# One encoder block on Trainium2: the work around the output projection goes to VectorE, weights are read earlier, and second products start from a copy of the first

## The chip, the cores and the metric

One core of one Trainium2 chip runs the whole program. The metric is the device time of one execution in microseconds (us), taken as the median of several runs. TensorE (PE) multiplies matrices out of SBUF into PSUM, which has eight banks of 128 x 512 fp32 numbers. VectorE (DVE), ScalarE (ACT) and GpSimd (POOL) work element by element; POOL does not touch PSUM. SyncE (SP) starts the transfers between the chip's main memory and SBUF. Each engine works through its own queue in order, and semaphores hold an instruction until what it needs is there.

## The reference

The input is 1024 tokens of width 1024, in front of which 16 meta tokens are set; all numbers are fp32. Two kinds of attention run in parallel on the normed input (four heads of differential attention, branch A; eight heads of windowed attention with sinks, branch B). They are merged by gates, projected, and followed by a SwiGLU feed-forward network (FFN) of width 2816:

```
merged = sigmoid(ga) * (y_a @ w_ba) + sigmoid(gb) * (y_b @ w_bb)     # 1024 x 512 @ 512 x 1024, twice
h = h + merged @ w_o                                                 # 1024 x 1024 @ 1024 x 1024
h = h + (silu(n @ w_gate) * (n @ w_up)) @ w_down                     # n = rms_norm(h, norm_ffn)
return rms_norm(h, norm_final)[:, N_META:]
```

The change touches the lines of the merge, of `w_o`, and of the first half of the FFN.

## The kernel before, in words

**Split numbers.** TensorE gets each fp32 operand as a high part and a low part. ScalarE copies the operand into the high part (rounded, line 112), and another engine, VectorE or POOL as the call says, subtracts that from the operand to make the low part (line 113). Both are done by `split(hi, lo, src, lo_eng)`. A product is then three matmuls: high by high, high by low, low by high. One matmul here is 128x128 by 128x512.

**Seven products for eight.** The projection and the FFN's products cut each matrix in quarters and use seven products of quarters in place of eight (Winograd's form). With the left side A (the merged rows) and the right side W: P1 = a11 w11, P2 = a12 w21, P6, P5 and P7 multiply sums of quarters, P3 and P4 a quarter by a sum. P1 + P2 is one quarter of the result; P6, P7 and P4 are added into the bank that holds P1, P3 into that which holds P5. The sums are element by element work for VectorE and POOL.

**Branches.** For each o of 0 to 7 (128 columns of the merge) and each half (512 tokens), `gated` reads a gate from main memory, takes its sigmoid and multiplies y by a 128-column piece of the branch's weights (12 matmuls) into a PSUM bank. Branch B runs first, with its result times the gate stored into a quarter (`merged(o, half)`); then branch A, in the order `order_a`, with its result times the gate (VectorE, line 887) added on POOL (line 888). `load_wo` reads quarters of `w_o`, 1 MB each.

**Output projection.** `right_o(p, j)` and `left_o(p, j)` split the two sides of product p, step j; `left_t` does so for the left side of P7 and P4. The steps run P1, P2, P6, P5, P3, four steps of four banks (`set1`, `set2`, `sets_o[5]`) and three matmuls each; then P7 and P4 bank by bank (`product_t`). After a product's last step, `out_add` (line 921) adds its banks to the rows `h2`. `ahead(n)` prepares the operands eight steps before they are used. When a block of 128 rows is complete, `norm_f` norms it, and `turn_f` transposes it on TensorE into two PSUM banks ("a turn"), from which ScalarE and VectorE make the FFN's operands, high and low part. Turns 0 to 4 stand between the last products of the projection (`TURN_O`), turns 5 to 7 among the first FFN products (`TURN`). From the second half of the tokens, a turn also makes the sums for P5, P6, P7 and P4 (lines 1080 to 1084), which `split_t` splits.

**FFN, first half.** The 2816 columns are 11 blocks fp of 256; i is 0 for the gate's weights and 1 for the up weights. `weights` reads and sums a block's weights and splits them, `product_f` multiplies (12 matmuls for each of seven p) into the banks b1, b2 and b3. For fp 0 to 3 (N_EARLY) P1 and P2 of all come first, since they need only half of the tokens, and the rest later; there the order for fp 1 to 3 is P1, P2 of i = 0, then P1, P2 of i = 1. From fp 4 on it is P1 of both i, P2 of both i, and so on. For fp below N_KEPT P1's bank is kept until P6 is added; for the others ScalarE copies P1 to SBUF and back. `result` evacuates: silu for i = 0, a multiplication with it for i = 1.

**Order.** On TensorE the order of the program text is kept. For the other engines and for SP a planner simulates the program and writes each engine's queue in the order in which its simulation starts the instructions. Buffers of one tag go round: a tile waits until the readers of the one before it in the same place are done. All PSUM tiles of these stages have one tag with eight banks:

```
def ps_bank(name):
    return bank(psum3, "bank", name, 8)
```

The functions that the diff touches, with the line numbers of the profile:

Of the kernel before, what the change touches and what calls it, by code (L numbers as in the profile page):

```python
# [60 lines left out]
S_TMP = 2  # L61
C_BUFS = 8
STAGGER = 3
# [7 lines left out]
def encoder_block(ctx: ExitStack, tc: tile.TileContext, x, meta, norm_mix, w_in, lq1, lk1, lq2, lk2,  # L71
# [746 lines left out]
    def ya(j, b, tk):  # L818
        return ya_t[j][:, b] if tk.start else ya0[:, b, j]

    def load_wo(w, row, col):
# [31 lines left out]
    late_pool, close_late = pool("late_pool", "right")  # L853
    gffn = row(late_pool, norm_ffn, D, "gffn")
    first_f = [late_pool.tile([P, 1024], F32, name=f"first_f{i}") for i in range(2)]
    w21 = late_pool.tile([P, 4, 512], F32, name="w21")
    load_wo(w21, 1, 0)


    tt_v, tt_p = nc.vector.tensor_tensor, nc.gpsimd.tensor_tensor  # L860
    t2 = [None, None]
    rights, lefts = {}, {}

    def right_o(p, j):
        if p == 6:
            src = t2[j // 2][:, j % 2 * 512:j % 2 * 512 + 512]
        else:
            src = w11[:, j] if p in (1, 5) else w21[:, j] if p in (2, 4) else m2[:, (3, 7).index(p), j]
        ob = rights[p, j] = late_pool.tile([P, 2, 512], F32R, tag="ob_o", name=f"ob_o{p}_{j}", bufs=8)
        split(ob[:, 0], ob[:, 1], src, nc.vector)  # L870

    def left_o(p, j):
        oa = lefts[p, j] = op_tile(f"oa_o{p}_{j}")
        split(oa[:, 0], oa[:, 1], {1: a11, 2: a12, 6: a11, 5: asum, 3: a12}[p][:, j], nc.gpsimd)

    def left_t(p, u):

        oa = lefts[p, u] = op_tile(f"oa_o{p}_{u}").rearrange("p a (c n) -> p a c n", n=P)
        split(oa[:, 0], oa[:, 1], {7: a21, 4: a22}[p][:, :, u * P:(u + 1) * P], nc.gpsimd)


    order_a = [(o, 0) for o in range(6)] + [(0, 1), (6, 0), (1, 1), (7, 0)] + [(o, 1) for o in range(2, DC)]
    for n, (o, half) in enumerate(order_a):
# [4 lines left out]
        nc.gpsimd.tensor_tensor(merged(o, half), gt, merged(o, half), ALU.add)  # L888
        if n < 4:
            right_o(1, n)  # L890
        elif n < 8:
            right_o(2, n - 4)
            left_o(1, n - 4)
        elif n < 12:
            if n > 9:
                left_o(2, n - 10)
        elif n < 14:
            left_o(2, n - 10)
            if n == 12:
                m2 = block_pair(2, "m2", F32)  # L900
                w22, w12 = m2[:, 0], m2[:, 1]
                load_wo(w12, 0, 1)
                load_wo(w22, 1, 1)
    close_ya()
    close_ypool()


    h2pool, close_h2 = pool("h2pool")

    def h2_tile(name):  # L910
# [3 lines left out]
    for t in range(NT):  # L914
        h2.append(h2_tile(f"h2_{t}"))
        nc.sync.dma_start(h2[t], x[t * P:(t + 1) * P, :])
    h2_d = [dram.tile([P, D], F32, name=f"h2_d{t}") for t in range(NT)]

# [136 lines left out]
    def turn_f(t):  # L1055
# [5 lines left out]
        for b in range(2):  # L1061
            pt = four(ps_bank(f"ptn_f{t}_{b}"))
            for c in range(4):
# [38 lines left out]
    set2 = [ps_bank(f"po_2_{u}") for u in range(4)]  # L1102
    sets_o = {1: set1, 2: set2, 6: set1}

    def product_o(p, j, u):
        oa, ob = lefts[p, j], rights[p, j]
        for k, (a, b) in enumerate(((0, 0), (0, 1), (1, 0))):
            nc.tensor.matmul(sets_o[p][u], oa[:, a, u * P:(u + 1) * P], ob[:, b, :],  # L1108
                             start=(p in (1, 2, 5) and j == 0 and k == 0),
                             stop=(p in (2, 3) and j == 3 and k == 2), skip_group_check=True)  # L1110
# [8 lines left out]
    def ahead(n):  # L1119
# [5 lines left out]
        else:  # L1125
            right_o((7, 4)[n // 4 - 3], n % 4)
            left_t(*((7, 0), (7, 1), (4, 0), (4, 1), (7, 2), (7, 3), (4, 2), (4, 3))[n - 12])

    for n, (p, j) in enumerate(steps_o):
        if (p, j) == (5, 0):  # L1130
            sets_o[5] = sets_o[3] = [ps_bank(f"po_5_{u}") for u in range(4)]
# [11 lines left out]
        for k in (n - 1, n) if last else (n,):  # L1143
            ahead(k)
            if k < 4:
                tt_v(a12[:, k], a12[:, k], a11[:, k], ALU.subtract)
            elif k < 8:
                tt_p(w21[:, k - 4], w21[:, k - 4], t2[(k - 4) // 2][:, k % 2 * 512:k % 2 * 512 + 512], ALU.subtract)
            elif k < 12:
# [3 lines left out]
    for n, (p, u) in enumerate(((7, 0), (7, 1), (4, 0), (4, 1), (7, 2), (7, 3), (4, 2), (4, 3))):  # L1153
        product_t(p, u)
# [5 lines left out]
    prepare(2 * 2)  # L1160
    close_late()
    close_keep()

# [22 lines left out]
    def product_f(fp, p, i):  # L1186
# [4 lines left out]
        late = N_KEPT <= fp < N_EARLY  # L1191
        if p in (1, 2, 5) or (late and p == 6):
            u[which] = ps_bank(f"pg_{nm}_{p}")
        ps = u[which]
# [3 lines left out]
        for c in range(4):  # L1198
            for n, (x, y) in enumerate(((0, 0), (0, 1), (1, 0))):
                nc.tensor.matmul(ps, op[:, x, c, :], b[:, y, c, :], start=(p in (1, 2, 5) and c == 0 and n == 0),  # L1200
                                 stop=(p in (4, 2, 3) and c == 3 and n == 2), skip_group_check=True)
        g = st.setdefault(("c", fp), {})

        def result(key, src, other=None):
# [8 lines left out]
            else:  # L1213
                if other is not None:
                    both = p_tile(f"p2_{nm}") if late and key == "11" else other
                    nc.vector.tensor_tensor(both, src, other, ALU.add)
                    src = both
                nc.vector.tensor_tensor(g[key], g[key], src, ALU.mult)

        if p in (1, 5):  # L1220
            u[p] = p_tile(f"p{p}_{nm}")
            nc.scalar.copy(u[p], ps)
# [64 lines left out]
    def product_d(p, j, us_):  # L1287
        oa, ob = ops["d", (p, j)]
        if BANKS[p] not in sets:
            sets[BANKS[p]] = [ps_bank(f"pd_{p}_{u}") for u in range(4)]  # L1290
        ps = sets[BANKS[p]]
# [127 lines left out]
```

## Time and profile before

| | us |
|---|---|
| median of 3 runs | 1462.16 (1461.48 to 1463.27) |
| the profiled execution | 1462.58 |
| its span, first to last instruction | 1460.8 |
| TensorE busy | 1435.5 (98%) |
| VectorE busy | 925.3 (63%) |
| ScalarE busy | 673.4 (46%) |
| POOL busy | 553.2 (38%) |
| mean granted TensorE clock | 0.995 of full speed |

In the rows of the profile, L12 is line 12 of the kernel; `m<-gt,m` is a tile written from two tiles (numbers left out); x4 is a count. A bracket behind a row of the order of time gives how long the engine stood before it, and which instruction ended that. PE is TensorE's matmuls and PEld its weight loads, which overlap them. A matmul's shown duration is longer than the pace, since one begins before the last has ended.

### The profile page before, as it was taken

Reading aid. Unit: us, or ns where it says so; the run is one execution under the profiler, and the core shown is the slowest. Engines: PE = TensorE matmul, PEld = TensorE weight load, DVE = VectorE, ACT = ScalarE, POOL = GpSimd, SP = SyncE. Lnnn points to the kernel's source line nnn. Section 1 sums busy time; section 2 is a strip of 40 time slices with the busy share of each in tenths; the row PEclk is TensorE's granted clock in tenths of the full one; section 3 lists DMA queues with packets and bytes.
Section 4 is the critical chain, followed back from the end, with each engine's and each line's share of the span. In section 5 each row is a group of like instructions: output and inputs, shape, how many; then the busy total and the mean of one; then the engine's idle time right before and its main releaser. Section 6 shows DMA issues by size and latency. Waiting matters only on the chain.

```text
span 1460.8 us, 21057 instructions
## 1 busy us (share of the span) xinstructions
PE 1435.5 (98%) x7327; PEld 1230.6 (84%) x7327; DVE 925.3 (63%) x1724; ACT 673.4 (46%) x1267; POOL 553.2 (38%) x512
## 2 busy tenths in 40 slices
PE   8999999999999999999989989999999999999997
PEld 7998989988898999888878868888888888788886
DVE  7456326628686868436698876655555554787667
ACT  6356336525555556355335633433333333444454
POOL 4143223313323232222876365554444542000444
PEclk9999999999999999999999999999999999999999
DMA  7334452372424251096421623432233323954333
GB/s 238 91 96 114 120 128 88 77 223 83 146 74 145 74 153 66 37 304 215 144 101 79 174 95 115 144 124 100 99 104 107 102 94 108 347 191 140 124 126 141
DMA packets 158618, 191.02 MB, mean 131 GB/s; under 512 B 16096, under 2 KB 103584, under 8 KB 158512
## 3 DMA queue, kind: packets, MB, share of 16 engines
q1 hardware_dynamic: 158512, 189.68, 40.6%
q8 instruction: 58, 0.95, 0.3%
q14 instruction: 48, 0.39, 0.1%
HBM read 129.14 MB, written 53.94 MB: 125 GB/s over the span
## 4 chain that ended last, share of the span: by engine, by line
PE 82%; DVE 6%; issue 4%; POOL 4%; DMA 2%; ACT 1%; SPq 1%; POOLq 0%; DVEq 0%; ACTq 0%
PE pg L1200 26%; PE pp_g L200 11%; PE pd L1294 8%; PE aps L607 4%; PE apy L649 3%; PE pp_va L200 3%; PE pp_ka L200 3%; PE pp_qb L200 3%; PE pp_qa L200 3%; POOL oa L113 3%; PE po L1108 2%; PE ppa L551 2%; PE apt L636 2%; PE bpt L338 2%; PE bpy L344 2%
## 5 line engine op out<-in xcount | busy, mean ns | idle before, releaser
L1200 PE MATMUL pg<-t,wop 128*128 128x512 f32 x1056 | 242.4, 389 | 0.0
L1200 PEld LDWEIGHTS pg<-t,wop 128*128 128x128 f32 x1056 | 198.2, 188 | 41.2
L113 POOL TENSOR_TENSOR wop<-wf,wop 128x512 fp32r<-128x512 f32 x122 | 165.7, 1360 | 172.6 <-ACT wop L112 161.7
L1294 PE MATMUL pd<-ob,oa 128*128 128x512 f32 x924 | 210.2, 389 | 1.5 <-DVE ob L113 1.1
L1294 PEld LDWEIGHTS pd<-ob,oa 128*128 128x128 f32 x924 | 173.3, 188 | 38.2 <-DVE ob L113 1.5
L1200 PE MATMUL pg<-b,wop 128*128 128x512 f32 x792 | 186.2, 393 | 5.2 <-ACT ts L1084 3.3
L1200 PEld LDWEIGHTS pg<-b,wop 128*128 128x128 f32 x792 | 149.3, 189 | 38.0 <-ACT ts L1084 3.7
L113 POOL TENSOR_TENSOR wl_c<-w_c,wh_c 128x1024 fp32r<-128x1024 f32 x32 | 77.7, 2427 | 162.5 <-ACT wh_c L112 138.3
L112 ACT ACTIVATE wop<-wf 128x512 fp32r<-128x512 f32 x128 | 80.5, 633 | 79.8 <-PE pg L1200 53.9
L113 POOL TENSOR_TENSOR oa<-ra,oa 128x512 fp32r<-128x512 f32 x33 | 44.1, 1336 | 171.4 <-ACT oa L112 170.0
L618 ACT ACTIVATE as<-as,amn 128x1040 f32<-128x1040 f32 x64 | 74.5, 1165 | 72.7 <-DVE amn L613 72.4
L200 PE MATMUL pp_g<-hT_hi,wh_c 128*128 128x512 f32 x256 | 101.3, 396 | 0.0
L200 PE MATMUL pp_g<-hT_lo,wh_c 128*128 128x512 f32 x256 | 100.9, 394 | 0.0
L200 PE MATMUL pp_g<-hT_hi,wl_c 128*128 128x512 f32 x256 | 100.9, 394 | 0.0
L112 ACT ACTIVATE oa<-ra 128x512 fp32r<-128x512 f32 x77 | 48.6, 632 | 107.8 <-PE pd L1294 52.7
L607 PE MATMUL aps<-ak,aq 128*128 128x352 f32 (+1 forms) x384 | 92.6, 326 | 0.0
L607 PEld LDWEIGHTS aps<-ak,aq 128*128 128x128 f32 x384 | 69.6, 188 | 14.0
L974 DVE TENSOR_TENSOR s<-wf,wf 128x512 f32<-128x512 f32 x20 | 18.3, 916 | 96.7 <-DMA wf<-in_w_ff_up_dram 53.3
L613 DVE CUSTOM_DVE_ANT_0 as<-aps,dist,amn 128x352 f32<-128x352 f32 (+1 forms) x128 | 71.2, 563 | 10.2 <-PE aps L607 8.1
L325 POOL TENSOR_SCALAR bs<-bs,bdn 128x432 f32<-128x432 f32 (+1 forms) x64 | 37.1, 601 | 87.6 <-DVE bdn L323 65.3
L621 POOL TENSOR_SCALAR as<-as,adn,neglam 128x1040 f32<-128x1040 f32 x32 | 39.0, 1219 | 75.2 <-DVE adn L619 75.2
L315 DVE CUSTOM_DVE_ANT_0 bs<-bps,tbx,nsink 128x432 f32<-128x432 f32 (+1 forms) x64 | 38.4, 624 | 41.6 <-PE bps L313 38.5
(275 smaller groups left out, 3134.8 us busy)
## 6 DMA issues: line engine op xcount, KB each, us to landing
ra<-aop SPq DMA_DIRECT2D x77, 256.0 KB, 2.6
w_c<-in_w_in_dram SPq DMA_DIRECT2D x33, 512.0 KB, 4.1
wf<-in_w_ff_gate_dram SPq DMA_DIRECT2D x25, 512.0 KB, 3.6
wf<-in_w_ff_up_dram SPq DMA_DIRECT2D x25, 512.0 KB, 3.6
aop<-as SPq DMA_DIRECT2D x44, 256.0 KB, 2.1
aop<-c SPq DMA_DIRECT2D x33, 256.0 KB, 2.0
g_d<-gate_stage SPq DMA_DIRECT2D x32, 256.0 KB, 2.0
gt<-g_d SPq DMA_DIRECT2D x32, 256.0 KB, 3.7
```

The costliest lines, as they stand in the source:

```text
L112: nc.scalar.activation(hi, src, AF.Copy)
L113: lo_eng.tensor_tensor(lo, src, f32(hi), ALU.subtract)
L200: nc.tensor.matmul(ps[:, :n], a[:, c, :], b[:, c, at:at + n], start=(c == 0 and i == 0), stop=(c == DC - 1 and i == 2))
L315: nc.vector.tensor_tensor_reduce(st[:, r, :W], ps[:, :W], tb, 2.0 ** -(4 * g + r + 1), nsink[:, 4 * g + r:4 * g + r + 1], ALU.add, ALU.min ...
L325: nc.gpsimd.tensor_scalar(st[:, r, :W], st[:, r, :W], dn[:, r:r + 1], 1.0, ALU.mult, ALU.mult)
L607: nc.tensor.matmul(ps[:, :n], qs[m][:, t * P:(t + 1) * P], ks[m][:, vv, k0:k0 + n], start=(vv == 0), stop=(vv == 1))
L613: nc.vector.tensor_tensor_reduce(s[m][:, a:b], ps[:, a - k0:b - k0], far_by, slope, low, ALU.add, ALU.min, mn[:, m, i + j:i + j + 1])
L618: nc.scalar.activation(s[m][:, 0:L], s[m][:, 0:L], AF.Exp, bias=low, scale=-1.0, accum_out=dn[:, m:m + 1])
L621: (nc.gpsimd if t % 4 in COMBINE_POOL else nc.vector).tensor_scalar(s[1][:, 0:L], s[1][:, 0:L], dn[:, 1:2], neglam, ALU.mult, ALU.mult)
L649: nc.tensor.matmul(py[:, cols], v[:kp, a, k, :], at_[:kp, k, b, :], start=(k == 0 and j == 0), stop=(k == 8))
L1200: nc.tensor.matmul(ps, op[:, x, c, :], b[:, y, c, :], start=(p in (1, 2, 5) and c == 0 and n == 0), stop=(p in (4, 2, 3) and c == 3 and n ...
L1294: nc.tensor.matmul(ps[u], oa[:, a, u * P:(u + 1) * P], ob[:, b, :], start=(p in (1, 2, 5) and j == 0 and k == 0), stop=(p in (2, 3, 4) and ...
```

## The change

- **Reads.** All four quarters of `w_o` but w22 are read beside branch B (w11 after o = 3, w12 after 4, w21 after 5). P1's right side is split there too, and w11 becomes w12 - w11 there, both on VectorE.
- **Sums and low parts.** The sums of the merged quarters are made beside branch A on VectorE, as they become complete, in another form (a21 = a11 - a21, asum = a22 - a21, a11 = asum + a11). All low parts of the projection's left sides, which were POOL's, are VectorE's, and so are the sums of fp 0 and the low parts of P1 and P2 for fp 2 and 3. w21's update goes from POOL to VectorE and to later steps.
- **Second products.** When P1 of the projection is complete, ScalarE copies its four banks to P2's, and P2 is added to that copy; the separate add of P1 to the rows goes. In the FFN's first half, P1 is copied to P2's bank (fp 0, 1 and from 4 on), or P2 is added in P1's own bank after that was copied to SBUF (fp 2 and 3), and the add of the two results goes.
- **Banks.** PSUM is divided: six banks of the old tag, and two of a new tag for half 1 of the branches, half of P2's and P5's banks in the projection, the turns, P5 in the FFN and half of one set in its second half. N_KEPT goes from 3 to 2.
- **Order.** The last products of the projection run 7,0 7,1 7,2 4,0 7,3 4,1 4,2 4,3 in place of 7,0 7,1 4,0 4,1 7,2 7,3 4,2 4,3, and the turns 0 to 3 stand one product later. The FFN norm's weights and the first FFN weights are read after branch A, into a pool of their own; copies of P5 and P6 are in another pool, of 16 buffers in place of 8.

```diff
 def ps_bank(name):
-    return bank(psum3, "bank", name, 8)
+    return bank(psum3, "bank", name, 6)
+
+def ps_bank_t(name):
+    return bank(psum3, "bank_t", name, 2)
...
+wopool, close_wo = pool("wopool", "right")
+w12, w21 = (wopool.tile([P, 4, 512], F32, name=f"w{n}") for n in ("12", "21"))
...
 def left_o(p, j):
     oa = lefts[p, j] = op_tile(f"oa_o{p}_{j}")
-    split(oa[:, 0], oa[:, 1], {1: a11, 2: a12, 6: a11, 5: asum, 3: a12}[p][:, j], nc.gpsimd)
+    split(oa[:, 0], oa[:, 1], {1: a11, 2: a12, 6: asum, 5: a11, 3: a12}[p][:, j], nc.vector)
...
-    ps = ps_bank(f"ppa_{o}_{half}_{i}")
+    ps = (ps_bank_t if half else ps_bank)(f"ppa_{o}_{half}_{i}")
...
-    if o == 3:
-        load_wo(w11, 0, 0)
+    if 3 <= o < 6:
+        load_wo(*((w11, 0, 0), (w12, 0, 1), (w21, 1, 0))[o - 3])
+    if o >= 4:
+        right_o(1, o - 4)
+        tt_v(w11[:, o - 4], w12[:, o - 4], w11[:, o - 4], ALU.subtract)
...
-    if n < 4:
-        right_o(1, n)
-    elif n < 8:
+    if 4 <= n < 8:
         right_o(2, n - 4)
         left_o(1, n - 4)
+    elif 10 <= n < 14:
+        left_o(2, n - 10)
+    if n in (6, 8, 10, 11):
+        tt_v(a21[:, o], a11[:, o], a21[:, o], ALU.subtract)
+    if n == 10:
+        w22 = obpools["w22"] = block_pair(2, "m2", F32)[:, 0]
+        load_wo(w22, 1, 1)
+    if n >= 12:
+        j = n - 12
+        tt_v(asum[:, j], a22[:, j], a21[:, j], ALU.subtract)
+        tt_v(a11[:, j], asum[:, j], a11[:, j], ALU.add)
...
-N_EARLY, N_KEPT = 4, 3
+N_EARLY, N_KEPT = 4, 2
...
-    tt = nc.vector.tensor_tensor if fp else nc.gpsimd.tensor_tensor
+    tt = nc.vector.tensor_tensor
...
-    split(op[:, 0], op[:, 1], src, nc.vector if (p in first and fp == 1) or (p == 6 and not fp) else nc.gpsimd)
+    split(op[:, 0], op[:, 1], src, nc.vector if (p in first and 0 < fp < N_EARLY) or (p == 6 and not fp) else nc.gpsimd)
...
-        pt = four(ps_bank(f"ptn_f{t}_{b}"))
+        pt = four(ps_bank_t(f"ptn_f{t}_{b}"))
...
-tt_v(asum[:, j], a21[:, j], a22[:, j], ALU.add)
-tt_p(a21[:, j], a11[:, j], a21[:, j], ALU.subtract)
-tt_v(a11[:, j], asum[:, j], a11[:, j], ALU.subtract)
-tt_v(w11[:, j], w12[:, j], w11[:, j], ALU.subtract)
 tt_v(t2[j // 2][:, j % 2 * 512:j % 2 * 512 + 512], w22[:, j], w11[:, j], ALU.subtract)
...
+order_t = ((7, 0), (7, 1), (7, 2), (4, 0), (7, 3), (4, 1), (4, 2), (4, 3))
...
-        if j == 3:
+        if (p, j) == (1, 3):
+            nc.scalar.copy(set2[u], set1[u])
+        elif j == 3:
             out_add(u + 4 * (p == 5), int(p > 2), sets_o[p][u])
...
-TURN_O = {1: 0, 2: 1, 3: 2, 4: 3, 6: 4}
+TURN_O = {2: 0, 3: 1, 4: 2, 5: 3, 6: 4}
...
-    if p in (1, 5):
-        u[p] = p_tile(f"p{p}_{nm}")
-        nc.scalar.copy(u[p], ps)
-    elif p == 6:
-        u[p] = p_tile(f"u2_{nm}")
+    if p == 1:
+        u["b2"] = ps if late else ps_bank(f"pg_{nm}_2")
+        if late:
+            u[1] = p_tile(f"p1_{nm}")
+        nc.scalar.copy(u[1] if late else u["b2"], ps)
+    elif p in (5, 6):
+        u[p] = c_tile(f"p{p}_{nm}")
         nc.scalar.copy(u[p], ps)
     elif p == 2:
-        result("11", ps, u[1])
+        result("11", ps)
```

More of the change, by code (lines that the diff above doesn't have):

```diff
@@ L61 @@
 S_TMP = 2
-C_BUFS = 8
+C_BUFS = 16
 STAGGER = 3
@@ L819, in ya, with right_o, left_o, left_t @@
         return ya_t[j][:, b] if tk.start else ya0[:, b, j]
+    tt_v = nc.vector.tensor_tensor
+    t2, obpools = [None, None], {}
+    rights, lefts = {}, {}
+    def right_o(p, j):
+        if p == 6:
+            src = t2[j // 2][:, j % 2 * 512:j % 2 * 512 + 512]
+        else:
+            src = {1: w11, 2: w21, 5: w11, 3: obpools.get("w22"), 7: w12, 4: w21}[p][:, j]
+        i = (1, 2, 6, 5, 3, 7, 4).index(p) % 2
+        ob = rights[p, j] = obpools[i].tile([P, 2, 512], F32R, tag="ob_o", name=f"ob_o{p}_{j}", bufs=4)
+        split(ob[:, 0], ob[:, 1], src, nc.vector)
+    def left_o(p, j):
+        oa = lefts[p, j] = op_tile(f"oa_o{p}_{j}")
+        split(oa[:, 0], oa[:, 1], {1: a11, 2: a12, 6: asum, 5: a11, 3: a12}[p][:, j], nc.vector)
+    def left_t(p, u):
+        oa = lefts[p, u] = op_tile(f"oa_o{p}_{u}").rearrange("p a (c n) -> p a c n", n=P)
+        split(oa[:, 0], oa[:, 1], {7: a21, 4: a22}[p][:, :, u * P:(u + 1) * P], nc.vector)
+    obpools[0] = wopool
     def load_wo(w, row, col):
@@ L852, in encoder_block @@
         split_ya(1, j)
[L853 to L873, printed above, removed]
-        split(oa[:, 0], oa[:, 1], {1: a11, 2: a12, 6: a11, 5: asum, 3: a12}[p][:, j], nc.gpsimd)
-    def left_t(p, u):
-        oa = lefts[p, u] = op_tile(f"oa_o{p}_{u}").rearrange("p a (c n) -> p a c n", n=P)
-        split(oa[:, 0], oa[:, 1], {7: a21, 4: a22}[p][:, :, u * P:(u + 1) * P], nc.gpsimd)
+    obpools[1], close_ob = pool("obpool", "right")
     order_a = [(o, 0) for o in range(6)] + [(0, 1), (6, 0), (1, 1), (7, 0)] + [(o, 1) for o in range(2, DC)]
@@ L916, in encoder_block @@
         nc.sync.dma_start(h2[t], x[t * P:(t + 1) * P, :])
+    gffn = row(late_pool, norm_ffn, D, "gffn")
+    first_f = [late_pool.tile([P, 1024], F32, name=f"first_f{i}") for i in range(2)]
     h2_d = [dram.tile([P, D], F32, name=f"h2_d{t}") for t in range(NT)]
@@ L1108, in product_o @@
             nc.tensor.matmul(sets_o[p][u], oa[:, a, u * P:(u + 1) * P], ob[:, b, :],
-                             start=(p in (1, 2, 5) and j == 0 and k == 0),
+                             start=(p in (1, 5) and j == 0 and k == 0),
                              stop=(p in (2, 3) and j == 3 and k == 2), skip_group_check=True)
@@ L1161, in encoder_block @@
     close_late()
+    close_ob()
+    close_wo()
     close_keep()
@@ L1191, in product_f @@
         late = N_KEPT <= fp < N_EARLY
-        if p in (1, 2, 5) or (late and p == 6):
-            u[which] = ps_bank(f"pg_{nm}_{p}")
+        if p in (1, 5) or (late and p == 6):
+            u[which] = (ps_bank_t if p == 5 else ps_bank)(f"pg_{nm}_{p}")
         ps = u[which]
@@ L1199, in product_f @@
             for n, (x, y) in enumerate(((0, 0), (0, 1), (1, 0))):
-                nc.tensor.matmul(ps, op[:, x, c, :], b[:, y, c, :], start=(p in (1, 2, 5) and c == 0 and n == 0),
+                nc.tensor.matmul(ps, op[:, x, c, :], b[:, y, c, :], start=(p in (1, 5) and c == 0 and n == 0),
                                  stop=(p in (4, 2, 3) and c == 3 and n == 2), skip_group_check=True)
@@ L1214, in result @@
                 if other is not None:
-                    both = p_tile(f"p2_{nm}") if late and key == "11" else other
-                    nc.vector.tensor_tensor(both, src, other, ALU.add)
-                    src = both
+                    nc.vector.tensor_tensor(other, src, other, ALU.add)
+                    src = other
                 nc.vector.tensor_tensor(g[key], g[key], src, ALU.mult)
-        if p in (1, 5):
-            u[p] = p_tile(f"p{p}_{nm}")
-            nc.scalar.copy(u[p], ps)
-        elif p == 6:
-            u[p] = p_tile(f"u2_{nm}")
+        if p == 1:
[5 more added lines that the diff above has]
+            u[p] = c_tile(f"p{p}_{nm}")
             nc.scalar.copy(u[p], ps)
         elif p == 2:
-            result("11", ps, u[1])
+            result("11", ps)
         elif p == 7:
@@ L1289, in product_d @@
         if BANKS[p] not in sets:
-            sets[BANKS[p]] = [ps_bank(f"pd_{p}_{u}") for u in range(4)]
+            sets[BANKS[p]] = [(ps_bank_t if BANKS[p] > 1 and u > 1 else ps_bank)(f"pd_{p}_{u}") for u in range(4)]
         ps = sets[BANKS[p]]
```

28 lines of the change are left out of this document (10 added, 18 removed).

## The prediction

> **What bounds the kernel now.** The page's first part comes first, then busy time by stage (the table of windows).
>
> ```profile
> PE 1435.5 (98%) x7327; PEld 1230.6 (84%) x7327; DVE 925.3 (63%) x1724; ACT 673.4 (46%) x1267; POOL 553.2 (38%) x512
> ```
>
> ```profile
> 723.00:813.00 90.00, 84.82 (x383) 69.33 (x383) 81.13 (x84) 41.11 (x75) 60.56 (x48) 0.96 0.23 88
> 813.00:856.00 43.00, 37.83 (x166) 30.00 (x165) 42.33 (x48) 25.41 (x47) 26.58 (x18) 0.96 0.56 159
> 856.00:1242.00 386.00, 386.00 (x1704) 319.57 (x1704) 212.34 (x233) 145.97 (x249) 184.91 (x136) 1.00 0.33 110
> ```
>
> The columns are the stretch, its length, then PE, PEld, DVE, ACT and POOL busy, the granted clock, the DMA share and GB/s. TensorE is the bound: no edit removes a matmul, so only its idle time and its clock can change. From 856 to 1242 there is none to win (386.00 busy of 386.00); its pace, 386.00/1704, is 0.2265 us a matmul, so a product of 12 takes 2.72. What can be won lies in the output projection (723 to 813) and the first FFN products (813 to 867), where VectorE is busy 81.13 of 90 and 42.33 of 43. TensorE's order of time there:
>
> ```profile
> 723.04 21.92 PE L1108 MATMUL po<-ob_o,oa_o 128*128 128x512 f32 x96
> 747.42 0.93 PE L1108 MATMUL po<-ob_o,oa_o 128*128 128x512 f32 x3 [2.46 <-DVE h L921]
> 749.83 34.97 PE L1108 MATMUL po<-ob_o,oa_o 128*128 128x512 f32 x141 [1.47 <-DVE h L921]
> ...
> 792.36 3.01 PE L1116 MATMUL po<-ob_o,oa_o 128*128 128x512 f32 x12 [1.25 <-DVE h L921]
> 795.21 1.04 PE L1065 MATMUL ptn_f<-ident,xn_f 128*128 128x128 f32 x8
> 796.00 3.01 PE L1116 MATMUL po<-ob_o,oa_o 128*128 128x512 f32 x12
> ...
> 813.24 5.73 PE L1200 MATMUL pg<-b,wop 128*128 128x512 f32 x24
> ...
> 825.94 14.32 PE L1200 MATMUL pg<-b,wop 128*128 128x512 f32 x60
> 840.92 3.03 PE L1200 MATMUL pg<-b,wop 128*128 128x512 f32 x12 [0.66 <-DVE c L1210]
> 847.25 7.36 PE L1200 MATMUL pg<-b,wop 128*128 128x512 f32 x24 [3.31 <-ACT ts L1084]
> 855.73 11.19 PE L1200 MATMUL pg<-b,wop 128*128 128x512 f32 x48 [1.12 <-DVE c L1210]
> 866.76 3.56 PE L1200 MATMUL pg<-t,wop 128*128 128x512 f32 x15
> ```
>
> Output projection: 7 products of 48 matmuls are 336, at 0.2265 76.1 us; six groups of eight transposes lie in it, 0.79 each (795.21 to 796.00), 4.7. That is 80.8 of the 90.2 from 723.04 to 813.24: 9.4 us lost. First FFN products: 16 of 12 matmuls, 43.5, and two groups of transposes, 1.6: 45.1 of the 53.5 to 866.76, 8.4 lost. Together 17.8, the most that this change could give. The clock has a share:
>
> ```profile
> 740.00:750.00 10.00, 6.07 (x26) 4.42 (x26) 9.96 (x11) 3.04 (x6) 6.11 (x5) 0.94 0.64 262
> 750.00:760.00 10.00, 10.00 (x33) 7.76 (x34) 10.00 (x11) 6.36 (x12) 10.00 (x7) 0.72 0.00 0
> ...
> 840.00:850.00 10.00, 6.04 (x21) 4.31 (x20) 10.00 (x11) 4.39 (x8) 10.00 (x8) 0.89 0.33 106
> 850.00:860.00 10.00, 8.88 (x37) 6.95 (x36) 9.27 (x8) 3.79 (x7) 6.51 (x5) 0.94 0.08 28
> ```
>
> After the waits of 2.46 and 1.47 it loses 0.06x10 + 0.28x10 = 3.4 us of full speed, after that of 3.31 1.1 + 0.6 = 1.7. So the projection loses 2.46 + 1.47 + 3.4 + 1.25 = 8.6 of its 9.4 by name, the FFN start 0.66 + 3.31 + 1.12 + 1.7 = 6.8 of its 8.4. The rest, 2.4, I leave standing.
>
> **VectorE and POOL (first gain).** Why is VectorE full? Its rows by group, two from these stages, one from the last stage, where POOL stands still, and what is taken from POOL:
>
> ```profile
> L113 DVE TENSOR_TENSOR ob_o<-m,ob_o 128x512 fp32r<-128x512 f32 x12 | 15.7, 1344 | 0.0
> L113 DVE TENSOR_TENSOR t<-kept,t 128x512 fp32r<-128x512 f32 x8 | 9.7, 1244 | 0.0
> L1023 DVE TENSOR_TENSOR wd_e<-wd_b,wd_a 128x512 f32<-128x512 f32 x11 | 7.5, 684 | 0.0
> L113 POOL TENSOR_TENSOR oa_o<-m,oa_o 128x512 fp32r<-128x512 f32 x28 | 40.6, 1461 | 16.4 <-ACT oa_o L112 16.4
> ```
>
> The same instruction on two SBUF operands takes 1.24 to 1.34 us beside POOL and 0.68 without it. The 28 low parts that POOL makes in 40.6 us cost VectorE about 28 x 0.68 = 19, and give back some 0.6 on each neighbour. In the projection VectorE loses four adds of P1 and eight sums moved beside branch A (the four weight differences that move beside branch B ran just ahead of 723), and gains the 20 low parts not moved to branch A and four sums of w21: 84 - 12 + 24 = 96 instructions. Beside branch A:
>
> ```profile
> 679.00:722.60 43.60, 43.29 (x192) 35.51 (x191) 31.40 (x36) 19.97 (x34) 31.86 (x23) 1.00 0.57 188
> ```
>
> There it gains eight low parts and twelve sums, 13.6 us, and loses P1's four right low parts and w11's four differences, 5.4: 31.4 + 8.2 = 39.6 of 43.6 before what POOL's freeing gives back, so it still fits. In the projection, at 0.68, with 0.6 more for each of the 7 row norms of double width, that is 69 us of about 81. So VectorE no longer ends last there. P6's bank then waits for ScalarE's copy, not for the add at line 921, and the order 7,0 7,1 7,2 4,0 puts two products between an add and the product that overwrites its bank, not one. I take out all 8.6 us. The copy set1 to set2 is hidden: the first of the four banks is complete three quarters of a step of 2.72 us, 2.04, before P2 starts, and a copy takes 0.59 (below): 1.4 spare, and a queue later by more than that costs the surplus once.
>
> In the FFN start eight adds of result 11 go, and sixteen instructions come from POOL (eight low parts, six sums of fp 0's P6 and two of P3). 48 + 8 = 56 at 0.68 is 38 of 45 us, so the 6.8 go as well: the bank that PE waited 3.31 for is no longer shared with products.
>
> **The reads beside branch B.** Two loads of 1 MB join a busy stretch:
>
> ```profile
> 640.00:650.00 10.00, 9.72 (x43) 7.71 (x43) 4.58 (x7) 5.72 (x10) 2.88 (x3) 1.00 1.07 361
> ```
>
> ```profile
> 634.78 11.53 PE L551 MATMUL ppa<-yb,wbhb 128*128 128x512 f32 x50
> ```
>
> ```profile
> 649.65 1.30 POOL L113 TENSOR_TENSOR wbhb<-wbrb,wbhb 128x512 fp32r<-128x512 f32 x1 [1.86 <-ACT wbhb L112]
> ```
>
> At 361 GB/s they take 5.8 us of the SP queue's transfers. Branch B's weights for o = 4 are ready at 651 and used at 634.78 + 4 x 5.44 = 656.5, a cover of 5.6. Cost: 0 to 1 us; I take 0, since the loads come after o = 3 and later weights lie further ahead. Gates (four buffers) and half 1's two banks have three products, 8.2 us, of slack, so also 0. The reads of gffn and the first FFN weights move behind branch A, past h2 on SP: needed only near 785, 60 us later, 0.
>
> **Second products on a copy (first cost).** The price of a copy, and where a product ends:
>
> ```profile
> 975.56 8.78 PE L1200 MATMUL pg<-b,wop 128*128 128x512 f32 x38
> ```
>
> ```profile
> 978.48 0.59 ACT L1222 COPY p<-pg 128x512 f32<-128x512 f32 x1 [2.03 <-PE pg L1200]
> ```
>
> P1 runs from 975.56 to 978.28, its copy to 979.07. From fp 4 on the other half's P1 stands between, P2 starts at 981.0: 1.9 spare, 0 cost, and the 386 us stay. But for fp 1 to 3 the order is P1, P2 of one half directly: PE must stand for 979.07 - 978.28 = 0.8 us, six times, 4.8 at least. Copying into PSUM isn't shown beside reading PSUM; SBUF to PSUM and PSUM to SBUF are both 0.59 (row L1197 of the products is 586 to 590 ns), so I take 0.59. How late can the copy be? Today's at fp 1:
>
> ```profile
> 832.94 0.58 ACT L1222 COPY p<-pg 128x512 f32<-128x512 f32 x1
> ...
> 836.50 0.59 ACT L1222 COPY p<-pg 128x512 f32<-128x512 f32 x1
> ```
>
> By 825.94 + 2.72 and + 3 x 2.72 those P1 end at 828.66 and 834.10: 4.3 and 2.4 us late, since ScalarE works its queue in order behind weight splits. So 0.8 to about 4.9 each. Today nobody waits for them; now PE would, and while it stands no new split is released. I take 1.0 each, 6.0, nearer the undisturbed row.
>
> **Two banks for transposes (second cost).** Today a turn takes any free bank of eight; then there are two:
>
> ```profile
> 790.88 1.07 ACT L1069 ACTIVATE b<-ptn_f 128x512 fp32r<-128x512 f32 x2
> 795.87 1.19 ACT L1072 COPY kept<-ptn_f 128x512 f32<-128x512 f32 x2 [3.93 <-DVE b L1070]
> ```
>
> The first turn's banks are read from 790.88 to 797.06, 6.2 us, with VectorE's low part in the middle (3.93 waited). A next turn comes back 2.72 + 0.79 = 3.5 later, of which 0.4 passes before its second bank: 0 to 3 us for each of four or five turns. Undelayed the chain is 0.59 + 0.68 + 0.59 = 1.9, and fits. Turns of the second half chain six steps, about 3.9, against 3.1 and twice 5.8. I take 4.0 in all.
>
> **Sum.** Off: 8.6 + 6.8 = 15.4. On: 6.0 + 4.0 = 10.0. Net -5.4. Against the profiled execution (span 1460.8, time 1462.58, 1.8 around it) that gives 1457.2; the median is 1462.16, 0.4 below that execution, and gives **1456.8**. 0.2% of it, what a measurement can tell from no change, is 2.9 us: up to 1459.2 is faster.
>
> **Rivals.**
> *All covered* (0.18): copies 0.8 each, no turn waits: -15.4 + 4.8 = -10.6, 1451.6. For: VectorE with 12 us free. Against: ScalarE is the queue that was late.
> *ScalarE late, slower* (0.20): place, the six pairs P1, P2 of fp 1 to 3. If the queue stays as today, each waits 0.6 more than the 4.3 and 2.4, on average 4.0: 24 + 4.0 - 15.4 = +12.6, 1474.8; halved, because standing lets it catch up, +0.6, and with waits of 2.5 each +3.6, 1465.8, which I take. It turns slower than no change from (15.4 - 4.0)/6 = 1.9 us a pair. Against: several of those delays came from VectorE's full queue, which is relieved.
> *Two banks cost the gain* (0.12): waits at today's chain, about 2 to 3 us for four turns, 9.4 in place of 4.0: 1462.2, no change.
> *VectorE becomes the bound* (0.04): if its mean stays 81.13/84 = 0.97, 96 instructions are 93 us, 12 over 80.8 where 9.4 were lost; with 10 of new waits and 6.8 won, 1468. Against: the 0.68 rows.
> *The clock* (0.04): six short waits 5.4 us apart might halve it.
>
> ```profile
> 854.00:858.00 4.00, 2.88 (x13) 2.06 (x12) 3.42 (x5) 2.29 (x5) 0.59 (x2) 1.00 0.19 70
> ```
>
> A wait of 1.12 inside these 4 us left it at 1.00; if each pair lost what the 3.31 wait lost, 1.7, that is 6 x 1.7 = 10.2: 1467. By the Trainium skill, "TensorE: Matmul & The Clock Gate", section on psum-queue depth-cycling, frequent short idling between groups of matmuls makes the clock swing and costs throughput; by that rule the time would be this rival's, and the row above speaks against it.
>
> **How the numbers follow.** The forecast itself has 0.42, 1452 to 1460. Faster is it and *all covered*, 0.60; same is *two banks*, 0.12; slower the other three, 0.28. The range goes from 1450, below *all covered*, to 1468, which takes in the slower ones but for the far end of the late queue.
>
> **What would show it.** Right: no wait on line 921 at P6 and no clock below 1.00 near 750; VectorE's low parts near 0.68 there; six waits of PE on the copy, about 1 us each, between 805 and 850; 856 to 1242's length unchanged. Wrong: waits of PE on copies of 2 us and more; waits of transposes on banks over 4 us in all; new gaps in the branches or in the products from fp 4 on.

## The result

The changed kernel takes 1474.88 us (median of 6 runs, 1472.36 to 1476.49) against 1462.53 for the kernel before (6 runs): ratio 1.0082, interval 1.0067 to 1.0097. It is slower by 12 us; the forecast was 5.4 us faster. Its profiled execution has a span of 1470.8 us, 10.0 more than before.

The page's busy times of the changed kernel, then its windows by stage (stretch, length, PE, PEld, DVE, ACT, POOL busy, clock, DMA share, GB/s):

```profile
PE 1439.6 (98%) x7327; PEld 1232.8 (84%) x7327; DVE 895.4 (61%) x1750; ACT 676.0 (46%) x1273; POOL 474.1 (32%) x460
```

```profile
679.00:723.00 44.00, 38.75 (x166) 31.65 (x165) 34.33 (x47) 18.12 (x32) 18.53 (x12) 0.93 0.31 101
723.00:813.00 90.00, 89.43 (x411) 73.20 (x409) 68.80 (x98) 45.16 (x82) 19.73 (x23) 1.00 0.29 109
813.00:870.00 57.00, 45.33 (x186) 35.59 (x187) 37.88 (x60) 29.05 (x52) 5.08 (x5) 0.91 0.42 125
```

VectorE and POOL do less than before (895.4 and 474.1 us, from 925.3 and 553.2), and the stretch of the projection (723 to 813) now runs almost without idle time (89.43 busy of 90) and at full clock. The loss stands on both sides of it: in branch A (clock 0.93) and in the first FFN products (45.33 busy of 57, clock 0.91). TensorE's order of time shows where:

```profile
679.47 35.52 PE L551 MATMUL ppa<-ya,wbha 128*128 128x512 f32 x156
720.24 10.28 PE L551 MATMUL ppa<-ya,wbha 128*128 128x512 f32 x36 [5.25 <-DVE gt L896]
730.36 54.56 PE L1118 MATMUL po<-ob_o,oa_o 128*128 128x512 f32 x240
...
797.21 1.26 PE L1078 MATMUL ptn_f<-ident,xn_f 128*128 128x128 f32 x8 [0.48 <-ACT kept L1085]
...
814.05 0.66 PE L1078 MATMUL ptn_f<-ident,xn_f 128*128 128x128 f32 x4 [1.09 <-ACT ts L1097]
814.46 5.73 PE L1215 MATMUL pg<-b,wop 128*128 128x512 f32 x24
...
825.55 1.11 PE L1078 MATMUL ptn_f<-ident,xn_f 128*128 128x128 f32 x4 [4.92 <-ACT ts L1097]
826.32 7.29 PE L1215 MATMUL pg<-b,wop 128*128 128x512 f32 x24
...
836.40 1.07 PE L1078 MATMUL ptn_f<-ident,xn_f 128*128 128x128 f32 x4 [2.35 <-ACT ts L1097]
837.12 4.29 PE L1215 MATMUL pg<-b,wop 128*128 128x512 f32 x12
842.08 5.74 PE L1215 MATMUL pg<-b,wop 128*128 128x512 f32 x24 [0.66 <-ACT pg L1239]
...
874.13 3.02 PE L1215 MATMUL pg<-b,wop 128*128 128x512 f32 x12 [0.68 <-ACT p L1239]
876.98 16.48 PE L1215 MATMUL pg<-t,wop 128*128 128x512 f32 x72
```

By starts of stages, against the prediction's rows of before: the 240 matmuls of P1 to P3 take 54.4 us (730.36 to 784.76), which is 240 at 0.2267: no wait at all. The projection takes 84.1 us to 814.46, where it took 90.2: 6.1 won. Branch A takes 50.9 (679.47 to 730.36) where 192 matmuls need 43.5: one wait of 5.25, and the half clock behind it. The FFN start takes 62.5 us (814.46 to 876.98) where it took 53.5: 9.0 lost, in three kinds of row: turns that wait for their bank (4.92, 2.35), six waits on copies (from 842.08 on, every 6.4 us for two products that need 5.44), and the clock. The windows by clock, cut at the changes of the granted clock and at PE's waits:

```profile
717.00:720.24 3.24, 0.00 (x1) 0.00 (x1) 3.24 (x7) 0.00 (x0) 0.00 (x0) 0.50 0.00 0
720.24:723.84 3.60, 3.60 (x9) 2.83 (x10) 3.02 (x5) 0.00 (x0) 3.58 (x2) 0.50 0.00 0
...
822.83:825.55 2.72, 0.00 (x0) 0.00 (x0) 2.72 (x6) 2.63 (x6) 0.00 (x0) 0.50 0.32 84
825.55:829.65 4.10, 4.10 (x12) 3.42 (x13) 4.10 (x8) 2.01 (x4) 0.00 (x0) 0.50 0.69 201
...
836.40:839.90 3.50, 3.50 (x11) 2.91 (x12) 3.50 (x7) 2.00 (x4) 0.00 (x0) 0.51 0.48 145
```

Twice the clock is halved while PE still stands, which costs nothing, and stays halved when it works again, which costs half of that time; the third time PE works throughout: 3.60/2 = 1.8 us in branch A, 4.10/2 + 3.50/2 = 3.8 in the FFN start. The 593.8 us of the span behind 876.98 are as long as before (594.0 behind 866.76).

**Branch A's wait.** Its last six products are all of half 1, which has two banks. VectorE's order of time while PE waits (from 715.0 to 720.2):

```profile
713.48 2.50 DVE L1107 TENSOR_TENSOR t<-m,m 128x512 f32<-128x512 f32 x4 [1.29 <-DMA m<-in_w_out_dram]
715.89 1.29 DVE L1161 TENSOR_TENSOR w<-m,w 128x512 f32<-128x512 f32 x2
717.10 0.68 DVE L905 TENSOR_TENSOR m<-m,m 128x512 f32<-128x512 f32 x1
717.70 1.28 DVE L1161 TENSOR_TENSOR w<-m,w 128x512 f32<-128x512 f32 x2
718.90 0.68 DVE L1163 TENSOR_TENSOR w<-w,t 128x512 f32<-128x512 f32 x1
719.51 0.68 DVE L896 TENSOR_TENSOR gt<-gt,ppa 128x512 f32<-128x512 f32 x1
```

Line 896 empties the bank. Ahead of it in the queue stand the sums that become possible when w22 lands: t2, and the updates of w12 and w21, which the program text has in the ninth step of the projection and later, some 40 us on; the planner took them as soon as its simulation had their inputs. The gate that this evacuation multiplies with was not late. Counted in order, it is the twelfth of branch A, and ScalarE had it ready at 708.83, before the product itself was complete (712.3):

```profile
708.20 0.63 ACT L860 ACTIVATE gt<-gt 128x512 f32<-128x512 f32 x1 [1.80 <-DMA gt<-g_d]
```

**A turn's bank.** Turn 5's second bank is written by 814.7 and wanted by turn 6 at 820.6. ScalarE and VectorE on it, and one row of ScalarE's queue between:

```profile
814.95 0.59 ACT L1082 ACTIVATE b<-ptn_f 128x512 fp32r<-128x512 f32 x1
...
820.32 1.15 ACT L112 ACTIVATE wop<-wf 128x512 fp32r<-128x512 f32 x2 [2.24 <-DMA wf<-in_w_ff_gate_dram]
...
824.93 0.57 ACT L1097 COPY ts<-ptn_f 128x512 f32<-128x512 f32 x1
```

```profile
818.05 0.68 DVE L1083 TENSOR_TENSOR b<-ptn_f,b 128x512 fp32r<-128x512 f32 x1
818.65 0.69 DVE L1094 TENSOR_TENSOR ptn_f<-ptn_f,ts 128x512 f32<-128x512 f32 x1
```

The last reader runs at 824.93 to 825.50, 10.8 us after the transposes. Six steps of about 0.6 are needed; the rest is waiting in two queues, behind splits, some of which wait for a transfer.

### The profile page after: what moved, and what is told of

The parts are those of the page before. It is cut to its first block, busy times and chain, and to the rows that moved or that the text cites. A ratio compares the mean times of both kernels' runs of the same rounds, so it can differ in the third digit from the quotient of the medians.

```text
span 1470.8 us, 20980 instructions
## 1 busy us (share of the span) xinstructions
PE 1439.6 (98%) x7327; PEld 1232.8 (84%) x7327; DVE 895.4 (61%) x1750; ACT 676.0 (46%) x1273; POOL 474.1 (32%) x460
## 4 chain that ended last, share of the span: by engine, by line
PE 82%; DMA 4%; issue 4%; POOL 3%; DVE 3%; ACT 2%; SPq 0%; POOLq 0%; ACTq 0%; DVEq 0%
PE pg L1215 28%; PE pp_g L200 11%; PE pd L1311 8%; PE aps L607 4%; PE po L1118 3%; PE apy L649 3%; PE pp_qb L200 3%; PE pp_va L200 3%; PE pp_ka L200 3%; PE pp_qa L200 3%; POOL oa L113 3%; PE apt L636 2%; PE bpt L338 2%; PE bpy L344 2%; PE bps L313 1%
## 5 line engine op out<-in xcount | busy, mean ns | idle before, releaser
L113 POOL TENSOR_TENSOR wop<-wf,wop 128x512 fp32r<-128x512 f32 x114 | 153.3, 1345 | 165.5 <-ACT wop L112 153.7
L113 POOL TENSOR_TENSOR oa<-ra,oa 128x512 fp32r<-128x512 f32 x33 | 44.1, 1337 | 170.8 <-ACT oa L112 169.3
L613 DVE CUSTOM_DVE_ANT_0 as<-aps,dist,amn 128x352 f32<-128x352 f32 (+1 forms) x128 | 71.3, 563 | 10.2 <-PE aps L607 8.1
```

The costliest lines, as they stand in the source:

```text
L113: lo_eng.tensor_tensor(lo, src, f32(hi), ALU.subtract)
L613: nc.vector.tensor_tensor_reduce(s[m][:, a:b], ps[:, a - k0:b - k0], far_by, slope, low, ALU.add, ALU.min, mn[:, m, i + j:i + j + 1])
```

## The experiments

Each is timed beside the kernel before, and differences below are to that; the changed kernel stands at +12.4. The medians are of 4 to 10 runs, and their intervals reach 2 to 3 us to either side. In the profiled executions branch A starts anywhere between 678.6 and 684.2 us, so single stages are compared by their lengths.

**Both branch halves on six banks.**

```diff
-    ps = (ps_bank_t if half else ps_bank)(f"ppa_{o}_{half}_{i}")
+    ps = ps_bank(f"ppa_{o}_{half}_{i}")
```

> The changed kernel, but both halves of the branches take their PSUM bank from the tag with six banks (the two others stay with the projection, the turns and P5). Bank theory: the wait of 5.3 us in branch A on the add at line 896 and the half clock behind it go, 6 to 7.5 us less than the changed kernel, about 1468. Queue theory (VectorE's sums of w22, placed ahead of the evacuation, and late gates are what holds PE): PE waits elsewhere in branch A or at P1, and the time stays within 2 us of 1474.9.

1467.3 against 1462.7: ratio 1.0034 (1.0017 to 1.0051), +4.6. Its order of time on TensorE:

```profile
681.10 43.68 PE L551 MATMUL ppa<-ya,wbha 128*128 128x512 f32 x192
724.62 54.56 PE L1118 MATMUL po<-ob_o,oa_o 128*128 128x512 f32 x240
```

Branch A's 192 matmuls run through in 43.5; the turns and copies behind are as in the changed kernel. With VectorE's queue as it is, the division of banks costs branch A 7.8 us (12.4 - 4.6; 7.4 by the stage's length).

This kernel and the two with one tag below do not compute the whole output. Probably part of P1 is missing, because P2 replaces instead of adding in part of the banks that ScalarE's copy was written to; that was not tested. The work and its order on TensorE are the same, so they are read as times. By the Trainium skill, "PSUM — Partial Sum Buffer", section "The four PSUM rules", a matmul without the start flag adds only where the bank's marks say that a matmul has written since they were last cleared, and a matmul with the flag clears the marks of its whole bank. That would be a reason for the change to keep the turns on banks of their own, and to let branch products run on all the banks that take copies; no run here shows the marks themselves.

**One tag of eight banks for everything** (both functions return `bank(psum3, "bank", name, 8)`).

> The changed kernel with one tag of eight banks again, for everything; all else as changed. Bank theory: the wait in branch A (5.3 and the clock, 6.6 in all) and the waits of the turns on banks (1.1 + 4.9 + 2.4 + 0.5 and the clock behind them, about 13) go, the six copies (5.7) stay: about 1456. ScalarE theory (its queue is late and whoever needs it waits, banks or not): the turns' waits turn up as waits of products on ScalarE's copies or on banks, less than 8 us off, 1467 or more.

1454.33, ratio 0.9948 (0.9933 to 0.9962), -8.4. No turn waits, branch A doesn't, and the six waits on copies are all that is left between 640 and 860 (the first is 1.2, the others 0.66 to 0.68). Beyond the branch's 7.8 the turns' two banks thus cost 13.0 (4.6 + 8.4), waits and half clock together.

**P1 of both i, then P2 of both i, for fp 1 to 3.**

```diff
-order_f += [(fp, p, i) for fp in range(1, N_EARLY) for i in range(2) for p in first]
+order_f += [(fp, p, i) for fp in range(1, N_EARLY) for p in first for i in range(2)]
```

> The changed kernel, with the order of the first FFN products of fp 1 to 3 made P1 of both i, then P2 of both i (as from fp 4 on), so that the other half's P1 stands between P1 and the P2 that adds to its copy. Copy theory: six waits of 0.95 each go, 5.7 us, about 1469. Rival: with all four products open at once fp 2 and 3 wait for banks instead, 1473 to 1475.

1467.1, ratio 1.0038 (1.0025 to 1.0051), +4.4: 8.0 less than the changed kernel.

```profile
844.04 27.54 PE L1215 MATMUL pg<-b,wop 128*128 128x512 f32 x120 [1.52 <-ACT pg L1239]
```

Ten products in a row, 27.4 us to 871.42 and no wait between, where six copies had stopped PE. One wait of 1.52 on a copy is left at their head, and the turns' waits are shifted (2.95 and 3.68 instead of 4.92 and 2.35). In the two traces the FFN start is 6.8 us shorter, 55.7 instead of 62.5. Of that the copies are 3.9 (six times 0.95, less the 1.8 that is lost at the one wait left), the turns' waits 0.6, and the clock 2.3: here it is halved once, from 824.2 to 827.6, of which PE works 2.8 us.

**Both edits.**

> Both edits together: one tag of eight banks, and P1 of both i ahead of P2 of both i for fp 1 to 3. If the three costs (branch A's two banks, the turns' two banks, the copies) add up, 1474.9 - 6.6 - 13 - 5.7 = 1450, faster than the kernel before by 12. If VectorE's or ScalarE's queue is what holds PE, the waits come back under other names and it stays above 1460.

1448.78, ratio 0.9913 (0.9896 to 0.9929), -13.9. The three costs add up: 7.8 and 13.0 by the times above and 5.7 by the rows of the copies are 26.5, and the two edits together win 26.3 (12.4 + 13.9). Between branch A and fp 0's P6 two waits are left, 1.11 in the FFN start and one that the changed kernel doesn't have, of P2 on the projection's copy:

```profile
734.70 43.81 PE L1118 MATMUL po<-ob_o,oa_o 128*128 128x512 f32 x192 [1.45 <-ACT po L1150]
```

**Four banks and four.** A division that keeps the turns apart from P1's banks, and computes all of the output.

```diff
-    return bank(psum3, "bank", name, 6)
+    return bank(psum3, "bank", name, 4)
-    return bank(psum3, "bank_t", name, 2)
+    return bank(psum3, "bank_t", name, 4)
-N_EARLY, N_KEPT = 4, 2
+N_EARLY, N_KEPT = 4, 1
-set2 = [(ps_bank, ps_bank_t)[u // 2](f"po_2_{u}") for u in range(4)]
+set2 = [ps_bank_t(f"po_2_{u}") for u in range(4)]
```

P5's set in the projection and the second and third set of the FFN's second half are all on the other four as well.

> The changed kernel with the eight banks divided four and four: half 0 of the branches, P1/P6 and the FFN's b1 and b2 on four; half 1, P2 and P5 of the projection, the turns and the FFN's b3 on the other four; so that P1's bank is kept for fp 0 only (N_KEPT 1). Bank theory: branch A's half 1 has four banks (a product later than the evacuation at 720 needs the same bank only at 720), a turn needs the banks of the turn before the last one, so both waits and the clock behind them go, the six copies stay: 1454 to 1457. Rival: ScalarE's or VectorE's queue holds the turns up by more than two products as well, and the FFN's four banks make P1 wait from fp 4 on: above 1462.

1452.74, ratio 0.9939 (0.9921 to 0.9957), -10.2. VectorE and TensorE:

```profile
718.35 0.68 DVE L896 TENSOR_TENSOR gt<-gt,ppa 128x512 f32<-128x512 f32 x1
```

```profile
678.60 43.68 PE L551 MATMUL ppa<-ya,wbha 128*128 128x512 f32 x192
```

The evacuation in branch A is as late as in the changed kernel, behind the same sums, and PE doesn't notice: with four banks it needs that one two products later.

**The same with the pairs apart.**

> The same with P1 of both i ahead of P2 of both i for fp 1 to 3: six waits of 0.95 less, 1448 to 1451. Rival: with four banks for b1 and b2 the four open products of fp 1 to 3 wait for one another, 1453 or more.

1449.11, ratio 0.9911 (0.9893 to 0.9929), -13.8: faster than the kernel before by that, and than the changed kernel by 26. The pairs apart win 3.6 here, not 5.7, since other waits come in their place.

```profile
PE 1430.1 (99%) x7327; PEld 1228.3 (85%) x7327; DVE 894.3 (62%) x1750; ACT 676.9 (47%) x1275; POOL 471.9 (33%) x460
```

```profile
818.26 13.97 PE L1215 MATMUL pg<-b,wop 128*128 128x512 f32 x60 [0.36 <-ACT c L1227]
833.54 19.33 PE L1215 MATMUL pg<-b,wop 128*128 128x512 f32 x84 [1.31 <-DVE c L1232]
```

Of the waits between branch A and fp 0's P6, three are left: 0.67, 0.36 and 1.31.

**w22's read later in the text**, after branch A's loop.

> The changed kernel (banks six and two) with w22 read after branch A instead of beside its product 10, so that the sums of w22, w12 and w21 cannot stand ahead of branch A's evacuations in VectorE's queue. If two banks alone hold branch A up: its wait stays near 5.3, time 1473 to 1476. If it takes the queue and the two banks together: the wait falls under 1.5, 1467 to 1469, unless w22's transfer then makes P6 late.

1476.14, ratio 1.0095 (1.0074 to 1.0116). This run tests nothing: the read was issued where it was before, as SP's queue shows, between gates of branch A that still ran, 27.9 us into branch A here and 27.7 in the changed kernel (707.18). The planner places a transfer when its simulation has what the transfer waits for, not by its line.

```profile
710.84 0.39 SPq L854 DMA_DIRECT2D m<-in_w_out_dram  x1
713.54 13.33 SPq L859 DMA_DIRECT2D gt<-g_d  x3
```

**The updates of w12 and w21 on POOL** (`nc.gpsimd` for lines 1161 and 1163).

> The changed kernel (banks six and two) with the updates of w12 and w21 (eight sums) on POOL, so that they no longer stand in VectorE's queue ahead of branch A's evacuation (there they run from 715.9 to 721.9, and the evacuation at 719.5). If the queue is the other half of the cause: the evacuation comes some 3 us earlier, the wait in branch A falls from 5.3 to 1.5 to 2.5, the half clock behind it shrinks, 1469 to 1472. If the gates are late by themselves or POOL's use holds VectorE as long: 1474 to 1476.

1475.28, ratio 1.0083 (1.0067 to 1.01): no change. VectorE's queue was shorter by eight sums, of which five stood ahead of the evacuation, but not earlier:

```profile
712.87 5.73 DVE L1107 TENSOR_TENSOR t<-m,m 128x512 f32<-128x512 f32 x4 [0.76 <-DMA m<-in_w_out_dram]
```

t2's four sums took 5.73 us beside POOL's, where they took 2.50, and the evacuation came at 720.19 (719.51 in the changed kernel).

**w22 in memory that comes free after branch A** (a tile of the pool behind h2), so that its read and its sums do come later.

> The changed kernel (banks six and two) with w22 in memory of its own that comes free only when branch A's gates and weights are done, so that its read, and the sums of t2, w12 and w21 with it, really come after branch A (in e7_w22_late the read was issued at the same place as in the changed kernel, so that run did not test this). If two banks alone hold branch A up: the wait of 5.3 stays, 1473 to 1476. If it takes the sums in VectorE's queue and w22's transfer ahead of the gates as well: the wait falls below 1.5, 1466 to 1469, with at most 1 us more at P6.

1464.69, ratio 1.0006 (0.9993 to 1.0019), 11 us less than the changed kernel, with two banks for half 1 as there:

```profile
680.09 44.02 PE L551 MATMUL ppa<-ya,wbha 128*128 128x512 f32 x192
```

```profile
732.68 2.48 DVE L1106 TENSOR_TENSOR t<-w,m 128x512 f32<-128x512 f32 x4
```

Branch A takes 43.9, and t2 is in time for P6, which doesn't wait. So it took both: two banks, and a queue that put w22's sums ahead of the evacuation. Either remedy is enough. (w22's transfer also came ahead of gates in the changed kernel, but the gate in question was ready all the same, as shown above.) The two traces differ by 6.6 of the 11 us: branch A is 7.0 shorter, and the FFN start 2.4, since turn 7's wait falls from 2.35 to 1.00 and brings no half clock; the projection is 1.3 longer, with a wait of P2 of 0.61 for its copy, and 1.5 are spread over the rest. Why turn 7's wait fell was not tested, and what the medians differ by beyond the traces isn't explained.

**The left low parts on POOL again.**

```diff
-    split(oa[:, 0], oa[:, 1], {1: a11, 2: a12, 6: asum, 5: a11, 3: a12}[p][:, j], nc.vector)
+    split(oa[:, 0], oa[:, 1], {1: a11, 2: a12, 6: asum, 5: a11, 3: a12}[p][:, j], nc.gpsimd)
...
-        split(oa[:, 0], oa[:, 1], {7: a21, 4: a22}[p][:, :, u * P:(u + 1) * P], nc.vector)
+        split(oa[:, 0], oa[:, 1], {7: a21, 4: a22}[p][:, :, u * P:(u + 1) * P], nc.gpsimd)
```

> The changed kernel with the low parts of the projection's left sides (28 of P1 to P4) on POOL again, all else as changed. If POOL's use is what slows VectorE: VectorE's instructions on two SBUF operands between 730 and 790 go from about 0.7 to over 1.0 us, PE waits in P1 to P3, where it has no wait now, and the time rises by 2 to 8 us, 1477 to 1483. If the relief of VectorE came from the copy of P1 and the moved sums alone: within 1.5 us of 1474.9.

1472.78, ratio 1.007 (1.0054 to 1.0086), an interval that overlaps the changed kernel's. VectorE's rows and TensorE's:

```profile
L113 DVE TENSOR_TENSOR ob_o<-w,ob_o 128x512 fp32r<-128x512 f32 x8 | 9.7, 1227 | 2.6 <-ACT ob_o L112 2.6
```

```profile
731.40 54.56 PE L1118 MATMUL po<-ob_o,oa_o 128*128 128x512 f32 x240
```

The same subtraction takes 1.23 us with POOL at work (0.69 in the changed kernel), as expected; but P1 to P3 still run without a wait, and the time is no higher. VectorE has room for the slower form. Over the projection, from P1's start to the FFN's first product, it is busy 63.5 us in 72 instructions here and 64.5 in 93 in the changed kernel. In order, the windows of the kernel before, the changed kernel and this one (VectorE is the third busy time):

```profile
723.04:813.24 90.20, 85.02 (x385) 69.56 (x384) 81.33 (x84) 41.11 (x75) 60.52 (x48) 0.96 0.23 88
730.36:814.46 84.10, 82.48 (x385) 67.79 (x384) 64.54 (x93) 45.98 (x84) 17.07 (x20) 1.00 0.31 113
731.40:815.54 84.14, 82.45 (x386) 67.80 (x384) 63.46 (x72) 46.14 (x84) 44.22 (x40) 1.00 0.31 113
```

**The copy of P1 alone**, put into the kernel before.

```diff
-            if j == 3:
+            if (p, j) == (1, 3):
+                nc.scalar.copy(set2[u], set1[u])
+            elif j == 3:
```

> The kernel before with one part of the change alone: P1 of the projection is copied to P2's banks by ScalarE and P2 is added to it, in place of the add of P1 to the rows. Sums, low parts, banks and FFN are as before. If the copy alone ends P6's wait: 2.46 + 1.47 and the 3.4 of half clock go, 1455 to 1457. If VectorE's fullness is the bound, P6's operands or banks are late all the same: the waits come back as waits on the low parts, 1460 to 1463.

1471.79, ratio 1.0056 (1.0039 to 1.0073), +8.9: slower than either expectation. TensorE from P2 on, and ScalarE's order of time (the profiled execution is the slowest of its four, 1476.70):

```profile
752.35 46.60 PE L1108 MATMUL po<-ob_o,oa_o 128*128 128x512 f32 x192 [12.96 <-ACT po L1139]
```

```profile
751.18 0.63 ACT L112 ACTIVATE oa_o<-m 128x512 fp32r<-128x512 f32 x1 [2.79 <-DVE m L1096]
751.71 2.04 ACT L1139 COPY po<-po 128x512 f32<-128x512 f32 x4
```

Its 48 matmuls of P1 ended at 739.4; the copy ran at 751.7, behind splits of P6's operands that waited for VectorE's sums. P6 no longer waits, since P2 has waited 13.0 us ahead of it. Where these sums are made in the projection, the copy is worse than the add that it replaces.

## Why the prediction was wrong

The sum had -15.4 of gains and +10.0 of costs. What each measured:

- **Projection's waits, -8.6: right.** P6's wait and its half clock went: P1 to P3 took 61.6 us (723.04 to 784.64) and take 54.4, 7.2 won where the prediction had 2.46 + 1.47 + 3.4 = 7.3. (By rows the clock's part is 2.9: it was halved from 748.8 to 755.6, and PE stood until 749.83, so 0.5 of the 3.4 is counted twice.) The wait of 1.25 behind the first turn went too. The stage as a whole won only 6.1, since 2.4 us went to turns on banks there (0.48, 1.09 and stretched transposes).
- **Why VectorE had room: wrong.** The prediction let the low parts' move from POOL end the fullness. Low parts beside POOL do take 1.2 instead of 0.7 us, but giving them back to POOL leaves VectorE's busy time where it was, 63.5 and 64.5 us in the projection against 81.3 before, and costs no time. So the room came with what else left the stage: twelve of VectorE's instructions (four adds of P1, and eight sums that are now made beside branch A), and some of POOL's own (44.2 us busy against 60.5 even with the low parts back). The copy alone doesn't do it: with it P2 waits 13 us. That the sums together with the copy are enough was not run by itself. The forecast of 69 us with 96 instructions came close (64.5 with 93), but the move that it was to come from turned out not to matter.
- **FFN start's waits, -6.8: right.** None of the rows of before comes back. With one tag of eight banks the FFN start takes 52.0 us: 45.1 of matmuls and turns, some 6 of waits on copies, and under 1 left.
- **Copies of fp 1 to 3, +6.0: right.** 0.95 a pair, 5.7 in all, and ScalarE was in time at each. So the rival "ScalarE late", whose 1474.8 at its far end is close to the measured time, had the time and not the cause.
- **Turns, +4.0: mis-sized.** They cost 13.0. The prediction gave a turn of the second half a chain of about 3.9 us against 5.8 of room between the FFN's products, so no wait there; the chain took 10.8, in two queues, and that is where 4.92 and 2.35 come from. The rival "two banks cost the gain" had the mechanism, with 9.4 of waits; the rows show 8.8 (0.5, 1.1, 4.9, 2.4). Left out by both was the clock, 3.8 us behind these two waits, of the kind that the prediction had just counted for the kernel before.
- **Half 1's two banks, 0: wrong.** The prediction gave them "three products, 8.2 us, of slack". That holds in branch B, where halves alternate. Branch A's order ends with six products of half 1 in a row, where a bank is wanted again after one product, 2.72 us. With the sums of w22 ahead of the evacuation that cost 7.8. In the kernel before sums of w22 stood in the same place; the row of VectorE there that ends the longest block, with an evacuation behind it at 728.62, is

```profile
722.92 5.77 DVE L1150 TENSOR_TENSOR m<-m 128x512 f32<-128x512 f32 x4
```

  There eight banks covered it, and no wait showed.
- **The reads beside branch B, 0, and the products from fp 4 on, 0: right.** Branch B takes 43.6 us from 635.91 to 679.47 (44.1 before), and 593.8 us behind 877 answer 594.0.

So two steps failed, both on banks: the turns at 4.0 in place of 13.0, and half 1's two banks at 0 in place of 7.8. Either alone would have turned the sign of -5.4 (+3.6 and +2.4). With all costs as measured the prediction's own sum is -15.4 + 5.7 + 13.0 + 7.8 = +11.1.

By stages of the two traces it is: projection -6.1 (it holds its turns' waits), branch A +6.8, the FFN start +9.0, before branch A +0.5, behind -0.2: +10.0, the difference of the spans. The medians differ by 2.4 more, which no trace shows.

## What to carry to other kernels

When buffers are divided, count for each tag the longest run of its users in the order that is really used, and hold the time to come round against the lateness that the trace already shows behind the old buffers; slack that hid it does not show as a wait. A dependence turned from one engine's queue to another's (an add into a copy) is worth what stands ahead of it in that queue: the projection's copy was free in the changed kernel, made P2 wait 0.6 and 1.5 us in two others, and 13 where the sums stood ahead of it. Moving a line does not move an instruction where a planner orders by readiness; change what it must wait for, and look in the trace whether it moved.

## What the runs showed of the hardware

A few microseconds of waiting cost some more in clock. The granted clock fell to 0.50 some 2 us into the waits of 5.25 and 4.92 us and stayed there for 6.8 (717.00 to 723.84, 822.83 to 829.65); behind the wait of 2.35, which ended at 836.40, it was halved for 3.4 more. The six waits of 0.7 us, 6.4 us apart, left it at 1.00:

```profile
850.00:860.00 10.00, 9.32 (x41) 7.40 (x40) 5.26 (x8) 2.87 (x5) 0.00 (x0) 1.00 0.26 82
```

So the rival of short waits that halve the clock fell here. The length of a wait alone doesn't decide: with the pairs apart the wait of 2.95 us halved the clock for 3.4 (824.2 to 827.6), while that of 3.68 left it at 1.00, during it and in the 7.6 us behind it:

```profile
832.70:836.38 3.68, 0.00 (x1) 0.00 (x0) 3.14 (x6) 2.24 (x5) 0.00 (x0) 1.00 0.24 54
836.38:844.00 7.62, 6.14 (x28) 4.82 (x28) 7.17 (x12) 3.70 (x8) 0.00 (x0) 1.00 0.67 219
```

ScalarE's copy from PSUM to PSUM, which no row of before had shown, takes 0.54 to 0.60 us for 128x512, like one from PSUM to SBUF (0.57 to 0.59).
